# Two chunks of weights instead of one multiplied with the first half of the tokens as a stage opens

## The chip, the cores and the metric

The kernel runs on one core of one Trainium2 chip. The metric is the device time of one execution in microseconds; the median of three runs of the kernel before is 2975.34 us.

## What is computed

512 tokens of width 1024 go through four stages, each of which norms its input, multiplies it with wide weights and adds its result to the stream:

```python
h = rmsnorm(x, norm_mix_g)                      # stage 1, "mix"
proj = h @ w_in                                 # gated linear attention, sliding-window attention, gates
x = x + merged @ w_out
x = x + peer_layer(rmsnorm(x, norm_ffn_g), ...) # stage 2, "peer"
# peer: qp = xn @ w_pq ; top 16 of 128 keys per half and head ; 16384 experts, gelu, weighted sum
x = x + rms_norm(gated_deltanet(rms_norm(x, pre0)), post0)   # stage 3, "gdn"
x = x + rms_norm(short_conv(rms_norm(x, pre1)), post1)       # stage 4, "sconv"
# short_conv: u, b, c, z = split(h @ w_in, 4) ; (b * conv(c * u) * silu(z)) @ w_out
```

## The kernel before, in words

Matrix products are made nearly exact: a float32 operand is split into a high part (rounded for the matrix engine, PE) and a low part (what is left), and `mm3` (L210 to L212) issues three products, high x high, high x low, low x high.

Weights come in chunks of 1024 x 256, each in two parts that `wchunk` (L81) prepares: SP's queue loads a part into `wraw` (L91), the scalar engine (ACT) makes the high part `whi` (L92), and the vector engine (DVE) subtracts to get the low part `wlo` (L95). In some stretches every n-th part is subtracted by GpSimd (POOL); `share["every"]` is that n and 0 means never. In stage 1 it is 1 for the first chunk, in stage 3 it is 2 while the first products run, and in the openings of stages 2 and 4 it is 0. The pools hold three raw parts and three pairs of high and low parts, so a part's conversion waits until an earlier part has been used. These three instructions carry a priority of 4000 places ahead.

A slab is a buffer of 16 KB in each partition; there are seven, under one tag, and a slab goes to whichever tile is first written when one is free. A stage's stream holds four: `x`, the scaled tokens `x1s` to `x4s`, and the normed transposed tokens in high and low parts, `x1h`, `x1l` and so on.

As a stage opens, the 512 tokens come from the stage before in two halves of 256. `norm` (L171) takes a tile of 128 tokens: DVE scales it by its reciprocal root (L180; the root is made on POOL, L122 and L124), PE transposes it in blocks (L185), DVE multiplies by the gains (L188), ACT makes the high part (L190) and DVE the low part (L191). `first_feat` (L193) multiplies chunk 0: the first half of the tokens with both its parts (2 x 24 products of 256 columns), then the second half is normed if it isn't yet, then its 2 x 24 products. The later chunks go through `proj_feat`, 2 x 24 products of 512 columns each.

The instruction order on each engine is planned ahead of the run: a planner with a model of costs takes, on each engine, the earliest instruction in the program (with its priority) that is ready by that model. In stage 3 (and in parts of stage 1) PE's order is the program's own (`manual_schedule`). PSUM has five banks under the tag `ps` and three under `pp`; the products of a chunk go to `pp`.

What is made of the first results differs: stage 1 copies them (L314 to L316), stage 2 copies them (L855), multiplies with keys (L860) and selects the top 16 of each on DVE (L865 to L869), stage 3 convolves (L1070, L1072), stage 4 multiplies and convolves (L1697 on).

## Time and profile before

| | us |
|---|---|
| median of three runs | 2975.34 (2971.92 to 2978.11) |
| profiled execution | 2977.74 |
| its span on the core | 2976.0 |
| PE busy in the span | 2859.2 |
| DVE, ACT, POOL busy | 1978.8, 1213.2, 683.0 |
| mean granted clock of PE | 0.987 |

The span runs from the first to the last instruction. Busy times of different engines overlap. A wait of PE is time in which PE had an instruction in line whose data or buffer was not there; the row names the engine and line that released it last.

### The profile page before, as it was taken

Reading aid. Unit: us, or ns where it says so; the run is one execution under the profiler, and the core shown is the slowest. Engines: PE = TensorE matmul, PEld = TensorE weight load, DVE = VectorE, ACT = ScalarE, POOL = GpSimd, SP = SyncE. Lnnn points to the kernel's source line nnn. Section 1 sums busy time; section 2 is a strip of 40 time slices with the busy share of each in tenths; the row PEclk is TensorE's granted clock in tenths of the full one; section 3 lists DMA queues with packets and bytes.
Section 4 is the critical chain, followed back from the end, with each engine's and each line's share of the span. In section 5 each row is a group of like instructions: output and inputs, shape, how many; then the busy total and the mean of one; then the engine's idle time right before and its main releaser. Section 6 shows DMA issues by size and latency. Waiting matters only on the chain.

```text
span 2976.0 us, 43447 instructions
## 1 busy us (share of the span) xinstructions
PE 2859.2 (96%) x16530; PEld 2516.2 (85%) x16530; DVE 1978.8 (66%) x3806; ACT 1213.2 (41%) x2089; POOL 683.0 (23%) x592
## 2 busy tenths in 40 slices
PE   8999999999889998999999999999999998999998
PEld 6989778888789998888889898787878898888888
DVE  3357765499998875777788887757856665444432
ACT  3534573322355554333333333466344453323222
POOL 1000110001342311333545544125621212000000
PEclk9999999999999999999999999999999999999999
DMA  3214224322366777999999999535522423223222
GB/s 134 79 33 143 97 96 159 116 88 89 135 222 230 262 250 268 321 340 359 311 347 339 347 330 338 178 87 133 162 104 96 128 96 108 92 99 121 99 94 78
DMA packets 208076, 528.67 MB, mean 178 GB/s; under 512 B 39929, under 2 KB 85593, under 8 KB 203514
## 3 DMA queue, kind: packets, MB, share of 16 engines
q1 hardware_dynamic: 145170, 326.17, 33.1%
q0 software_dynamic: 43168, 155.27, 14.6%
q10 hardware_dynamic: 19528, 44.44, 4.1%
q8 instruction: 130, 2.13, 0.3%
q14 instruction: 80, 0.66, 0.1%
HBM read 464.49 MB, written 61.33 MB: 177 GB/s over the span
## 4 chain that ended last, share of the span: by engine, by line
PE 61%; DVE 5%; ACT 2%; DMA 1%; issue 1%; POOL 0%; ACTq 0%; DVEq 0%; POOLq 0%
PE pp L210 13%; PE pp L211 13%; PE pp L212 13%; PE ps L212 5%; PE ps L211 5%; PE ps L210 5%; PE ps L1517 2%; PE ps L968 1%; PE ps L969 1%; DVE wlo L95 1%; PE ps L1547 1%; DMA gath<-in_peer_u_rows_dram,ge 1%; PE ps L1566 1%; DVE AB L963 0%; ACT whi L92 0%
## 5 line engine op out<-in xcount | busy, mean ns | idle before, releaser
L92 ACT ACTIVATE whi<-wraw 128x1024 fp32r<-128x1024 f32 x492 | 519.1, 1056 | 847.0 <-PE pp L211 583.1
L95 DVE TENSOR_TENSOR wlo<-wraw,whi 128x1024 fp32r<-128x1024 f32 x466 | 583.0, 1251 | 349.1 <-ACT whi L92 338.7
L212 PE MATMUL pp<-x2h,wlo 128*128 128x384 f32 (+2 forms) x1168 | 402.7, 345 | 21.0 <-DVE wlo L95 19.4
L210 PE MATMUL pp<-x2h,whi 128*128 128x384 f32 (+2 forms) x1168 | 405.9, 348 | 15.1 <-ACT whi L92 8.7
L211 PE MATMUL pp<-x2l,whi 128*128 128x384 f32 (+2 forms) x1168 | 402.4, 345 | 0.8 <-DVE x2l L191 0.8
L212 PE MATMUL ps<-whi,wtl 128*128 128x512 f32 x640 | 252.7, 395 | 0.0
L211 PE MATMUL ps<-wlo,wth 128*128 128x512 f32 x640 | 252.6, 395 | 0.0
L210 PE MATMUL ps<-whi,wth 128*128 128x512 f32 x640 | 252.4, 394 | 0.0
L762 POOL DMA_INDIRECT gath<-in_peer_v_rows_dram,ge x128 | 181.7, 1420 | 306.4 <-DVE gath L765 153.8
L762 POOL DMA_INDIRECT gath<-in_peer_u_rows_dram,ge x128 | 182.2, 1424 | 296.5 <-DVE acc L770 144.5
L212 PEld LDWEIGHTS pp<-x2h,wlo 128*128 128x128 f32 x1168 | 223.4, 191 | 29.5 <-DVE wlo L95 22.9
L210 PEld LDWEIGHTS pp<-x2h,whi 128*128 128x128 f32 x1168 | 224.1, 192 | 21.7 <-ACT whi L92 9.4
L211 PEld LDWEIGHTS pp<-x2l,whi 128*128 128x128 f32 x1168 | 223.7, 192 | 6.5 <-DVE x2l L191 1.4
L210 PE MATMUL pp<-x4h,whi 128*128 128x512 f32 (+1 forms) x528 | 202.9, 385 | 3.8 <-ACT x4h L190 3.8
L211 PE MATMUL pp<-x4l,whi 128*128 128x512 f32 (+1 forms) x528 | 203.0, 385 | 0.6 <-DVE x4l L191 0.6
L212 PE MATMUL pp<-x4h,wlo 128*128 128x512 f32 (+1 forms) x528 | 202.8, 384 | 0.0
L830 ACT ACTIVATE wth<-wt 128x384 fp32r<-128x384 f32 x128 | 67.2, 525 | 330.8 <-PE pp L211 187.1
L770 DVE SCALAR_TENSOR_TENSOR acc<-gath,w,acc 128x1024 f32<-128x1024 f32 x127 | 162.5, 1279 | 25.4 <-DMA gath<-in_peer_v_rows_dram,ge 25.1
L765 DVE SCALAR_TENSOR_TENSOR gath<-gath,grow 128x1024 f32<-128x1024 f32 x128 | 157.3, 1237 | 33.0 <-DMA gath<-in_peer_u_rows_dram,ge 32.4
L210 PE MATMUL pp<-x3h,whi 128*128 128x512 f32 (+1 forms) x400 | 165.1, 413 | 7.4 <-ACT x3h L190 5.7
L211 PE MATMUL pp<-x3l,whi 128*128 128x512 f32 (+1 forms) x400 | 154.8, 387 | 1.6 <-DVE x3l L191 1.6
L212 PE MATMUL pp<-x3h,wlo 128*128 128x512 f32 (+1 forms) x400 | 154.9, 387 | 0.0
(498 smaller groups left out, 6534.9 us busy)
## 6 DMA issues: line engine op xcount, KB each, us to landing
wraw<-in_peer_u_dram SPq DMA_DIRECT2D x128, 512.0 KB
wraw<-in_peer_v_dram SPq DMA_DIRECT2D x128, 512.0 KB
wraw<-in_sc_w_in_dram SPq DMA_DIRECT2D x64, 512.0 KB
wraw<-in_w_in_dram SPq DMA_DIRECT2D x52, 512.0 KB
Gd<-sgs ACTq DMA_DIRECT2D x24, 1024.0 KB
wraw<-in_gdn_w_in_dram SPq DMA_DIRECT2D x48, 512.0 KB
Gt<-Gd SPq DMA_DIRECT2D x48, 400.0 KB
Hd<-ht ACTq DMA_DIRECT2D x25, 384.0 KB
```

The lines of the kernel that those rows point to most:

```text
L92: S.activation(hi, raw, AF.Copy)
L95: (GP if pool_ else V).tensor_tensor(lo, raw, f32(hi), op=ALU.subtract)
L210: PE.matmul(p, lh, rh, start=first, stop=False, skip_group_check=skip)
L211: PE.matmul(p, lh, rl, start=False, stop=False, skip_group_check=skip)
L212: PE.matmul(p, ll, rh, start=False, stop=last, skip_group_check=skip)
L762: GP.indirect_dma_start(out=r, out_offset=None, in_=src, in_offset=bass.IndirectOffsetOnAxis(ap=idx3[:, k:k + 1], axis=0))
L765: V.scalar_tensor_tensor(r, r, 1.0, xn3, op0=ALU.mult, op1=ALU.mult, accum_out=h3[:, k:k + 1])
L770: V.scalar_tensor_tensor(acc3, r, w3[:, k:k + 1], acc3, op0=ALU.mult, op1=ALU.add)
L830: S.activation(wh, w, AF.Copy)
L968: PE.matmul(o, AB[:, 1, :, q], A2[:, 0, :, q], start=True, stop=False)
L969: PE.matmul(o, AB[:, 1, :, q], A2[:, 1, :, q], start=False, stop=True)
L1517: PE.matmul(out_, RQ[s_][:, c:c + P], rhs, start=True, stop=True)
```

## The change

`first_feat` takes two chunks. Chunk 0's four parts go into one slab `wx`, and their low parts are always made on POOL; chunk 1's go through the small pool as before. The first half of the tokens is multiplied with both chunks (4 x 24 products of 256 columns), then the second half is normed, then it is multiplied with both. It is a generator now and hands out each result as it is finished; the fourth result lies in a bank of the tag `ps`. All four stages take their first four results from it. In stage 1 the line that set `share["every"]` is gone.

```diff
--- before.py
+++ after.py
@@ -78,20 +78,24 @@
     raws = {"of": [wraw], "n": 0}
-    def wchunk(ap, name="w"):
+    def wchunk(ap, name="w", into=None):
         for i in range(NK // HK):
             raws["n"] += 1
             raw = raws["of"][raws["n"] % len(raws["of"])].tile([P, HK * 256], F32, name=name + "raw", tag="wraw")
-            hi = wsp.tile([P, HK * 256], F32R, name=name + "hi", tag="whi")
-            lo = wsp.tile([P, HK * 256], F32R, name=name + "lo", tag="wlo")
+            if into is None:
+                hi = wsp.tile([P, HK * 256], F32R, name=name + "hi", tag="whi")
+                lo = wsp.tile([P, HK * 256], F32R, name=name + "lo", tag="wlo")
+            else:
+                hi, lo = into[:, 2 * i], into[:, 2 * i + 1]
             with tc.high_priority(offset=WPRIO):
                 nc.sync.dma_start(raw, ap[:, i * HK * 256:(i + 1) * HK * 256])
                 S.activation(hi, raw, AF.Copy)
                 share["n"] += 1
-                pool_ = share["every"] and share["n"] % share["every"] == 0
+                pool_ = into is not None or share["every"] and share["n"] % share["every"] == 0
                 (GP if pool_ else V).tensor_tensor(lo, raw, f32(hi), op=ALU.subtract)
             yield i, hi, lo
@@ -190,21 +194,25 @@
                 S.activation(h, p, AF.Copy)
                 V.tensor_tensor(l, p, f32(h), op=ALU.subtract)
-        def first_feat(self, ap, order=(0, 1)):
-
-            w = [(m, *kview(x, NK)) for m, *x in wchunk(ap)]
-            pp = [pj() for m in range(2)]
+        def first_feat(self, aps, order=(0, 1)):
+            wx = s16([P, 4, HK * 256], F32R, name="x%dw" % self.n)
+            w = [kview(x, NK) for ap, o in ((aps[0], wx), (aps[1], None)) for m, *x in wchunk(ap, into=o)]
+            w = [tuple(x) for x in w]
+            pp = [pj(), pj(), pj(), ps()]
             for j in order:
                 s = slice(256 * j, 256 * j + 256)
                 if j == order[1] and 2 * j not in self.normed:
                     self.norm(2 * j)
                     self.norm(2 * j + 1)
-                for m, wh, wl in w:
+                for p, (wh, wl) in zip(pp, w):
                     for k in range(NK):
-                        mm3(pp[m][:, s], wh[:, k], wl[:, k], self.h[:, k, s], self.l[:, k, s],
+                        mm3(p[:, s], wh[:, k], wl[:, k], self.h[:, k, s], self.l[:, k, s],
                             j == order[0] and k == 0, k == NK - 1, True)
-            return pp
+                    if j == order[1]:
+                        yield p
     def mm3(p, lh, ll, rh, rl, first, last, skip=False):
         PE.matmul(p, lh, rh, start=first, stop=False, skip_group_check=skip)
@@ -310,9 +318,9 @@
             gng = cl("gla_norm_g", [P, 2])
             xh, xl = X.h, X.l
             gqk = s16([P, 8, 512], name="gqk")
+            first2 = X.first_feat([w1[0], w1[1]])
             for c in range(4):
-                share["every"] = c == 0
-                for m, p in enumerate(proj_feat(w1[c], xh, xl) if c else X.first_feat(w1[0])):
+                for m, p in enumerate(proj_feat(w1[c], xh, xl) if c > 1 else (next(first2) for _ in range(2))):
                     S.activation(gqk[:, 2 * c + m, :], p, AF.Copy)
             wgh = cp.tile([P, NK * 16], F32R, name="wgh")
@@ -846,9 +854,10 @@
             tk = s16([P, 4, 1024], name="tk")
             v5 = lambda x: x.rearrange("p (t h m k) -> p t h m k", t=NT, h=8, m=2)
             top, itop = v5(tk[:, 0]), v5(tk[:, 1].bitcast(U32))
+            first2 = X.first_feat([A["w_peer_q"][0], A["w_peer_q"][1]])
             for h in range(8):
-                for m, p in enumerate(proj_feat(A["w_peer_q"][h], xh, xl) if h else
-                                      X.first_feat(A["w_peer_q"][0])):
+                for m, p in enumerate(proj_feat(A["w_peer_q"][h], xh, xl) if h > 1 else
+                                      (next(first2) for _ in range(2))):
                     if h == 0 and m == 0:
                         V.scalar_tensor_tensor(xn3, X.x[:, 3, :], X.rs[:, 3:4], grow, op0=ALU.mult, op1=ALU.mult)
                     q = tq.tile([P, T], F32, name="pq", tag="pq", bufs=2)
@@ -1115,8 +1124,8 @@
                 nonlocal gk
                 if i == 0:
-                    gk = iter(X.first_feat(w1[0], (1, 0)))
-                elif i % 2 == 0:
+                    gk = X.first_feat([w1[0], w1[1]], (1, 0))
+                elif i % 2 == 0 and i > 2:
                     gk = proj_feat_steps(w1[i // 2], xh, xl, NK)
                 return next(gk)
@@ -1692,13 +1701,14 @@
             xh, xl = X.h, X.l
             parts = [(s16([P, NK, T], F32R, name="sh%d" % i), s16([P, NK, T], F32R, name="sl%d" % i))
                      for i in range(2)]
+            first2 = X.first_feat([w1[0], w1[1]])
             for m in range(16):
-                p, p2 = proj_feat(w1[2 * m], xh, xl) if m else X.first_feat(w1[0])
+                p, p2 = proj_feat(w1[2 * m], xh, xl) if m else [next(first2) for _ in range(2)]
                 u = t2("scu")
                 S.activation(u, p, AF.Copy)
                 V.tensor_tensor(u, u, p2, op=ALU.mult)
                 acc = conv_silu(u, cw[:, m, :], 3, t2)
-                p, p2 = proj_feat(w1[2 * m + 1], xh, xl)
+                p, p2 = proj_feat(w1[2 * m + 1], xh, xl) if m else [next(first2) for _ in range(2)]
                 V.tensor_tensor(acc, acc, p, op=ALU.mult)
                 z = t2("scz")
                 S.activation(z, p2, AF.Silu)
```

## Rows read from the trace of the kernel before

**Rows 1.** The page's busy times: engine, busy us, share of the span, instructions.

```profile
PE 2859.2 (96%) x16530; PEld 2516.2 (85%) x16530; DVE 1978.8 (66%) x3806; ACT 1213.2 (41%) x2089; POOL 683.0 (23%) x592
```

**Rows 2.** Waits of PE, whole span: waiter, releaser, total us, times, longest us.

```profile
PE ps L185 <- DVE x4s L180: 5.9, 1, 5.9
PE pp L210 <- ACT x2h L190: 5.8, 2, 3.4
PE pp L210 <- ACT x3h L190: 5.7, 2, 4.4
PE pp L210 <- ACT x4h L190: 3.8, 2, 2.5
```

**Rows 3.** Timeline, stage 2 opening, PE: start, us, instruction, idle before.

```profile
583.30 0.80 PE L210 MATMUL pp<-x2h,whi 128*128 128x256 f32 x2 [3.38 <-ACT x2h L190]
...
591.98 1.91 PE L185 MATMUL ps<-ident,x2s 128*128 128x128 f32 x16
...
596.26 0.74 PE L210 MATMUL pp<-x2h,whi 128*128 128x256 f32 x3 [2.37 <-ACT x2h L190]
```

**Rows 4.** Timeline, stage 2 opening, DVE and ACT.

```profile
579.60 1.22 DVE L95 TENSOR_TENSOR wlo<-wraw,whi 128x1024 fp32r<-128x1024 f32 x1
...
587.78 1.42 DVE L180 TENSOR_SCALAR x2s<-x,x2rs 128x1024 f32<-128x1024 f32 x2 [1.11 <-POOL x2rs L124]
...
601.56 1.06 ACT L92 ACTIVATE whi<-wraw 128x1024 fp32r<-128x1024 f32 x1 [2.96 <-PE pp L211]
...
602.52 0.58 ACT L855 ACTIVATE pq<-pp 128x512 f32<-128x512 f32 x1
...
604.35 0.30 DVE L865 MAX8 tk<-ps 128x8 f32<-128x128 f32 x1 [0.48 <-PE ps L860]
...
604.57 1.21 DVE L95 TENSOR_TENSOR wlo<-wraw,whi 128x1024 fp32r<-128x1024 f32 x1
```

**Rows 5.** Timeline, stage 3 opening.

```profile
1919.24 2.36 POOL L95 TENSOR_TENSOR wlo<-wraw,whi 128x1024 fp32r<-128x1024 f32 x1 [1.34 <-ACT whi L92]
...
1920.47 2.22 DVE L95 TENSOR_TENSOR wlo<-wraw,whi 128x1024 fp32r<-128x1024 f32 x1
...
1929.82 1.42 DVE L180 TENSOR_SCALAR x3s<-x,x3rs 128x1024 f32<-128x1024 f32 x2 [2.02 <-POOL x3rs L124]
...
1933.80 1.91 PE L185 MATMUL ps<-ident,x3s 128*128 128x128 f32 x16
```

**Rows 6.** Timeline, stage 4 opening.

```profile
2523.76 1.42 DVE L180 TENSOR_SCALAR x4s<-x,x4rs 128x1024 f32<-128x1024 f32 x2 [1.75 <-POOL x4rs L124]
...
2527.26 1.91 PE L185 MATMUL ps<-ident,x4s 128*128 128x128 f32 x16
```

**Rows 7.** Timeline, stage 1 opening.

```profile
25.61 1.27 DVE L191 TENSOR_TENSOR x1l<-ps,x1h 128x512 fp32r<-128x512 f32 x2
...
28.97 0.40 PE L210 MATMUL pp<-x1h,whi 128*128 128x256 f32 x2
...
34.73 0.40 PE L210 MATMUL pp<-x1h,whi 128*128 128x512 f32 x1
```

**Rows 8.** Timeline, stage 4, PE: products of 512 columns.

```profile
2863.67 0.39 PE L211 MATMUL pp<-x4l,whi 128*128 128x512 f32 x1
...
2872.05 0.39 PE L212 MATMUL pp<-x4h,wlo 128*128 128x512 f32 x1
```

**Rows 9.** Timeline of SP's queue: issues of weight parts, x of them merged.

```profile
556.08 25.10 SPq L91 DMA_DIRECT2D wraw<-in_w_peer_q_dram  x6
...
1901.46 0.36 SPq L91 DMA_DIRECT2D wraw<-in_gdn_w_in_dram  x1
...
2484.53 27.09 SPq L91 DMA_DIRECT2D wraw<-in_sc_w_in_dram  x6
```

**Rows 10.** Windows: length, PE, PEld, DVE, ACT, POOL busy, clock, DMA, GB/s.

```profile
600.00:720.00 120.00, 120.00 (x636) 105.07 (x635) 112.31 (x619) 33.59 (x44) 0.86 (x1) 1.00 0.29 96
720.00:1000.00 280.00, 247.07 (x1501) 233.26 (x1500) 254.87 (x505) 127.21 (x154) 107.65 (x60) 0.98 0.55 190
```

## The prediction

> **What bounds the kernel now.** The page's busy times come first: the matrix engine is busy 2859.2 of 2976.0 us, so 116.8 us are idle on it and nothing can be won elsewhere unless it first makes PE wait less [rows 1]. The second view is PE's own waits. The openings of the stages stand in it by name: PE waits for the first normed tokens of stage 2 and again for the second, 5.8 us in two waits of which the longest is 3.4, so 3.4 and 2.4; in stage 3 4.4 and 1.3; in stage 4 5.9 (for the scaled tokens), 2.5 and 1.3 [rows 2]. The question for this change is which of these waits a second chunk can cover. I therefore read the timelines of the openings, PE first and then the engines that feed it.
>
> Stage 2 (peer): the first-half products of chunk 0 start at 583.30, the transposes of the second half follow them at 591.98 without any idle, and only after the transposes does PE stand for 2.37 us until 596.26 [rows 3]. The scaled second half was there at 587.78 + 1.42 = 589.2, 2.8 us before PE asked for it [rows 4]. Stage 3 (gdn): ready at 1929.82 + 1.42 = 1931.2, asked for at 1933.80, 2.6 us to spare [rows 5]. Stage 4 (sconv): ready at 2525.2, asked for at 2527.26, 2.1 us to spare [rows 6]. Stage 1 (mix): the last part of the second half is done at 25.61 + 1.27 = 26.9 and its products begin at 28.97 [rows 7]. So in all four openings one chunk already covers the making of the second half. What is idle lies before the first product (more work behind it does not help) and between the transposes and the second-half products.
>
> **The change, part by part.**
>
> *The split.* Chunk 1 is now done as two halves of 256 tokens, 96 products where there were 48 of 512. In stage 1 the 48 half-width products from 28.97 to 34.73 take 5.76 us, 0.12 apiece [rows 7]; a full-width one takes (2872.05 - 2863.67) / 37 = 0.2265, 37 steps lying between these two rows [rows 8]. So 2 x 0.12 - 0.2265 = 0.0135 us more for each of 48, 0.65 us an opening. This is added PE work on an engine that is the bound, with nothing to hide it.
>
> *The order.* The norm of the second half stands in the program behind all first-half products, now 96 and no longer 48; the planner takes the earliest instruction that is ready, and in stage 3 PE follows the program outright. So the transposes come 48 x 0.12 = 5.76 us later, the second half lies ready that much longer, and the wait between transposes and second-half products stays where it is, since nothing is left on PE to put in it. Value: 0. Bounds: at best these waits go altogether, 2.4 + 1.3 + 1.3 = 5.0 us [rows 2]; at worst they are what they are. In stage 2 the wait is 1.1 us longer than in the other two because the vector engine was on other work; that work now falls under the 5.76 us, so I take 1.1 off there.
>
> *The large buffer.* One slab of seven takes chunk 0's four parts. Counting the slabs in use at each opening (stage 2: two of the merged input, four of the stream; stage 3: the stream's and the last H and Gt; stage 4: two parts, Y and the stream's x until its s, h and l are written) leaves one free when the parts arrive. Value 0; the other end is a rival below. The weight slots that chunk 0 no longer takes are refilled by chunk 1 and the first part of chunk 2 at the same releases, so the conversions that sit in the openings stay: the vector engine's subtraction at 579.60 is then that of a later part [rows 4], the one at 1920.47 likewise [rows 5]. Value 0; were they gone from the chain to the first product, at best 1.22 + 2.22 and, counting stage 4 as two like the first, 2.4, together 5.8 us; at worst one more falls into the chain, 1.2 an opening.
>
> *The engine of chunk 0's subtraction.* In stages 2 and 4 both parts, in stage 3 one of two, move from DVE to POOL: five instructions of about 2.36 us where DVE takes 1.22 [rows 4, 5]. POOL also makes the reciprocal roots of the norms, so a part that runs at the wrong time would hold these. But the parts are loaded early: the DMA queue issues stage 2's from 556.08, stage 3's second at 1901.46, stage 4's from 2484.53 [rows 9], some 20 us before the first products, and no slot of the small pool has to come free first any more. Value 0. The bound is a collision: beside POOL's 2.36 us DVE's subtraction took 2.22 instead of 1.22, 1.0 us more [rows 4, 5]. Five collisions would be 5.0 us by that row, and five whole POOL instructions 11.8.
>
> The Trainium skill (SBUF — State Buffer, section "SBUF: two separate sides") holds that the port pair that VectorE and GpSimd share is an exclusive lock, so that the second to come is blocked for the whole of the other's instruction. The trace nearly agrees: the DVE instruction began at 1920.47 and ended 1.09 us after POOL's end at 1921.60. By that rule each collision could cost up to what POOL had left to run, and it speaks against moving these subtractions.
>
> *The results come later in stage 2.* There DVE is nearly the bound: 112.31 of 120 us from 600 to 720 and 254.87 of 280 from 720 to 1000, where PE has 33 us idle [rows 10]. Its selection chain starts with the first result of chunk 0, which now has 5.76 us of chunk 1 in front of it. Against that: 1.1 of the wait above; ACT's copy of that result, which stood behind a weight conversion that waited for PE until 601.56 and so came at 602.52, while its 24 products, back to back, would be done at 596.26 + 24 x 0.12 = 599.1 (3.4 us, since the conversions in front of it no longer wait for chunk 0's slots); and the subtraction at 604.57, 1.21 us, that is then done before [rows 4]. 5.76 - 1.1 - 3.4 - 1.21 = 0.05; I take 1.0, as not all of the ACT wait need go. Bounds: -1 (the wait and the split alone) and +5.8 (nothing is paid back). In this stage DVE sets the end, so the split isn't added.
>
> *Sum.* Stages 1, 3, 4: 3 x 0.65 = 1.95; stage 2: 1.0. Together +3.0 us. The profiled execution took 2977.74 (2976.0 of span and 1.7 around it), so it would take 2980.7; it lies 2.4 above the median of the runs, 2975.34, and the forecast for the median is 2978.3. About 0.2% (6 us) is what a measurement of this kernel can tell from no change, so this is "no change".
>
> **The rivals.**
>
> A, fast: the weight work leaves the openings, and the planner finds the transposes ready and puts them in front of chunk 1's products. Then up to 5.8 + 5.0 us go and 3.0 come: 2975.3 - 7.8 = 2967.5; with the 5.8 alone, 2972.5. For it: the waits are there and chunk 1's halves would fit them exactly. Against it: the transposes stand later in the program, PE never lacks a ready product in front of them, and in stage 3 the order is fixed. The planner also sees other times throughout and may order stage 2's tightly shared DVE better.
>
> B, slow: POOL's subtractions fall into the chains of the openings and hold the norm's roots and DVE. It decides as soon as chunk 0's parts reach POOL after about 574, 1916 and 2502. Price 5.0 (the measured collision) to 11.8, with the sum above: 2983 to 2990. Against it: the early DMA issues [rows 9].
>
> C, slow: stage 2's chain is pushed by the whole 5.76 and pays nothing back, 5.76 + 1.95 = 7.7: 2983.0. For it: DVE's 94% there [rows 10]. Against it: the ACT wait that goes.
>
> D: the change doesn't do what it says, since a slab is not free in time. In stage 4 the parts would wait for the slab of the scaled tokens, free at 2527.26 + 1.91 = 2529.2 [rows 6], then take a POOL instruction: some 13 us against a first product at about 2518.7 (after the wait of 2.5). About 2991.
>
> **How the numbers follow.** The forecast's own case 0.45, A 0.25, B 0.13, C 0.12, D 0.05. A is faster by over 0.2% only in its full form, but I leave it its whole 0.25 for a planner that gains in stage 2; B, C and D are 0.30. Range: 2967 (all of A) to 2990 (B's upper end), which leaves D and what is beyond A outside.
>
> **What would show it.** After the change PE should begin the second-half transposes 14 to 15 us after the first product in stage 2 (8.7 now), without idle in front, and should still stand 1 to 2.5 us behind them in stages 2, 3 and 4. Chunk 1 should show as half-width products, 0.12 us each. POOL's subtractions should lie before 574, 1916 and 2502, and the first product of each opening should follow the end of the stage before as it does now, within 1 us. The first selection instruction of stage 2 should be about 2 us later. I am wrong if the first product of an opening moves by more than 2 us, if transposes stand between chunk 0's and chunk 1's first halves, or if stage 2 changes by more than 4 us from its first product to its end.

## The result

The changed kernel takes 2999.97 us (median of 4 runs, 2997.86 to 3003.56) where the kernel before, run beside it, takes 2975.78. The ratio is 1.0081, 95% interval 1.0069 to 1.0094: 24 us slower. The forecast was 2978.3 and its range ended at 2990. The profiled execution took 2999.29 us, span 2997.5.

The page's busy times, columns as in [rows 1]: PE has 10.7 us more to do and 10.8 us more in which it does nothing (2997.5 - 2869.9 = 127.6, against 116.8).

```profile
PE 2869.9 (96%) x16722; PEld 2531.9 (84%) x16722; DVE 1966.5 (66%) x3801; ACT 1209.4 (40%) x2086; POOL 700.0 (23%) x597
```

PE's waits over the whole span, to be held against [rows 2]. The wait of L1201 (g_sums, the column sums of the gates in stage 3) was not there before; stage 4's waits have grown, stage 2's have shrunk (from 5.8 for x2h to 2.9, but 2.7 for x2s is new).

```profile
PE ps L189 <- DVE x4s L184: 7.1, 1, 7.1
...
PE ps L1201 <- DVE sma L1197: 5.4, 1, 5.4
PE pp L218 <- ACT x4h L194: 4.9, 2, 3.6
PE ps L1149 <- ACT l2sq L1139: 3.4, 2, 2.2
PE pp L218 <- ACT x2h L194: 2.9, 2, 1.6
...
PE ps L189 <- DVE x2s L184: 2.7, 1, 2.7
```

The opening of stage 2 on PE, the answer to [rows 3] (start, us, instruction, idle before): the second transposes now stand 15.0 us behind the first product, with no idle in front, and the waits behind them are still there. That is what the prediction said. What it did not say is the rate. The last two rows, half-width products one behind the other, start 0.22 us apart, not 0.12.

```profile
583.52 0.80 PE L218 MATMUL pp<-x2h,x2w 128*128 128x256 f32 x2 [1.58 <-ACT x2h L194]
...
598.54 1.91 PE L189 MATMUL ps<-ident,x2s 128*128 128x128 f32 x16
601.75 0.50 PE L218 MATMUL pp<-x2h,x2w 128*128 128x256 f32 x2 [1.31 <-ACT x2h L194]
...
604.61 0.41 PE L218 MATMUL pp<-x2h,x2w 128*128 128x256 f32 x1
604.83 0.41 PE L219 MATMUL pp<-x2l,x2w 128*128 128x256 f32 x1
```

The first selection instruction, in [rows 4] at 604.35, is 5.6 us later, and DVE sat idle for 5.14 us in front of it. ACT's copy of the first result, from which the selection is made, had waited for PE (ACT, then DVE):

```profile
608.11 0.60 ACT L864 ACTIVATE pq<-pp 128x512 f32<-128x512 f32 x1 [4.01 <-PE pp L220]
```

```profile
609.96 0.30 DVE L874 MAX8 tk<-ps 128x8 f32<-128x128 f32 x1 [5.14 <-PE ps L869]
```

POOL's subtractions of chunk 0, which the prediction had put ahead of 574, 1916 and 2502, are here (POOL, the openings of stages 2, 3 and 4; in this run the first transposes of stage 3 come 3 us later than before, those of stage 4 16 us later):

```profile
580.88 5.66 POOL L99 TENSOR_TENSOR x2w<-wraw,x2w 128x1024 fp32r<-128x1024 f32 x2 [6.08 <-ACT x2w L96]
...
1927.18 4.69 POOL L99 TENSOR_TENSOR x3w<-wraw,x3w 128x1024 fp32r<-128x1024 f32 x2
...
2534.20 5.66 POOL L99 TENSOR_TENSOR x4w<-wraw,x4w 128x1024 fp32r<-128x1024 f32 x2 [4.60 <-ACT x4w L96]
```

On ACT the conversions that feed them stand between the second and the third write of x4h, in stage 4 as in the two others. The large buffer was made in the middle of the opening, from parts that had been loaded long before (SP issued the stage's first two parts at 2499.30 and 2500.77):

```profile
2532.11 1.06 ACT L194 ACTIVATE x4h<-ps 128x512 fp32r<-128x512 f32 x2
2533.07 2.00 ACT L96 ACTIVATE x4w<-wraw 128x1024 fp32r<-128x1024 f32 x2
2535.09 1.20 ACT L194 ACTIVATE x4h<-ps 128x512 fp32r<-128x512 f32 x2
```

DVE beside POOL in stage 4: the same operation of the output projection takes 1.28 us before POOL starts and 2.08 beside it, and the last x4l for which PE waits comes after it.

```profile
2529.63 1.28 DVE L1064 SCALAR_TENSOR_TENSOR x<-ygY,yr,x 128x1024 f32<-128x1024 f32 x1 [0.58 <-POOL yr L128]
...
2535.56 2.08 DVE L1064 SCALAR_TENSOR_TENSOR x<-ygY,yr,x 128x1024 f32<-128x1024 f32 x1
2537.55 1.28 DVE L195 TENSOR_TENSOR x4l<-ps,x4h 128x512 fp32r<-128x512 f32 x2
```

The Trainium skill (SBUF — State Buffer, section "SBUF: two separate sides") has a GpSimd instruction that reads SBUF and a DVE instruction with two SBUF inputs exclude each other: whichever starts first has the port pair for its whole length. The trace fits that nearly in size. POOL's 5.66 us are 2.35 and 3.35. The DVE operation, with its inputs in SBUF, began when the first of them had 1.0 us left, and grew by 0.8; the second was 1.0 longer than the first. x4l, with one input in PSUM, keeps its 0.64 us apiece.

**Stage 3 on PE.** Five rows of the changed kernel. The transposes and the first wait of 1.3 us are as before; ab_mm (at 1955.09) stands 33.1 us behind the first transposes instead of 25.5; and then PE has nothing left to put ahead of g_sums:

```profile
1943.38 1.91 PE L189 MATMUL ps<-ident,x3s 128*128 128x128 f32 x16
1946.60 0.38 PE L218 MATMUL pp<-x3h,x3w 128*128 128x256 f32 x1 [1.31 <-ACT x3h L194]
...
1974.02 0.95 PE L1149 MATMUL ps<-ones,l2sq 128*128 128x1 f32 x8
1980.33 0.69 PE L1201 MATMUL ps<-sma,c_tri 128*128 128x64 f32 x2 [5.36 <-DVE sma L1197]
1980.78 0.78 PE L218 MATMUL pp<-x3h,whi 128*128 128x512 f32 x1
```

In the kernel before, g_sums has no wait:

```profile
1969.37 0.41 PE L1192 MATMUL ps<-sma,c_tri 128*128 128x64 f32 x2
```

The window behind the wait, columns as in [rows 10]: the granted clock is 0.68, a mixture of the levels 1.2 and 2.4 GHz. The 24 full-width products from 1980.78 take 8.15 us; at 2.4 GHz 24 of them take 24 x 0.2265 = 5.4 [rows 8].

```profile
1980.00:1990.00 10.00, 9.67 (x37) 8.03 (x38) 1.19 (x8) 4.17 (x7) 0.00 (x0) 0.68 0.03 12
```

The wait is the sum of two changes. PE has less to put between ab_tok and g_sums, since result 3 is 24 half-width products now: from 1964.35 to 1974.97, 10.6 us, where the kernel before had 13.1 (1956.25 to 1969.37). And the chain between them on ACT and DVE takes longer, 15.7 us to the start of sma's last step where it took 12.1 (DVE, before and changed):

```profile
1968.36 0.21 DVE L1188 SCALAR_TENSOR_TENSOR sma<-sma,alog 128x64 f32<-128x64 f32 x1
```

```profile
1980.06 0.21 DVE L1197 SCALAR_TENSOR_TENSOR sma<-sma,alog 128x64 f32<-128x64 f32 x1
```

2.5 and 3.6 us, less the 0.8 us that the kernel before had to spare, give 5.3 of the 5.36. Why the chain takes longer stands on ACT. A function table is loaded whenever the chain's exponentials and the results' Silu alternate, three times (1.28 us each) up to the chain's last exponential in the kernel before and four times here, as result 2's Silu (L1137) is now planned between two of the exponentials. A weight conversion of 1.06 us and its wait of 0.94 stand there too, at 1967.80 (ACT, before and changed):

```profile
1956.99 1.28 ACT L1175 ACT_TABLE_LOAD   x1
...
1958.96 1.28 ACT L1128 ACT_TABLE_LOAD   x1
...
1963.80 1.28 ACT L1182 ACT_TABLE_LOAD   x1
```

```profile
1965.20 1.28 ACT L1184 ACT_TABLE_LOAD   x1
...
1966.62 0.25 ACT L1185 ACTIVATE sme<-sma 128x64 f32<-128x64 f32 x1
...
1968.88 1.28 ACT L1137 ACT_TABLE_LOAD   x1
1970.17 0.63 ACT L1137 ACTIVATE kq<-cva 128x512 f32<-128x512 f32 x1
1970.83 1.28 ACT L1186 ACT_TABLE_LOAD   x1
1972.12 0.26 ACT L1186 ACTIVATE sme<-sme 128x64 f32<-128x64 f32 x1
...
1975.06 1.28 ACT L1191 ACT_TABLE_LOAD   x1
```

The Trainium skill (ScalarE: Activation LUTs, section "What ACT_TABLE_LOAD costs") gives 1283 ns for the load, which the trace has, and 1380 ns more for draining, which it doesn't: the load at 1970.83 begins 0.03 us after the end of the instruction ahead of it, and the one behind it starts 0.01 us after its end.

One window from the first transposes of stage 3 to the first step of the triangular solve (W), which waits for everything the gates feed, in the kernel before and in the changed one:

```profile
1918.88:2111.90 193.02, 181.62 (x997) 150.39 (x997) 130.28 (x255) 112.47 (x173) 72.69 (x64) 0.97 0.52 130
```

```profile
1922.00:2125.20 203.20, 187.84 (x1040) 157.78 (x1041) 124.41 (x254) 109.10 (x170) 75.76 (x65) 0.94 0.49 125
```

10.2 us more: 4.0 of idle (15.4 against 11.4) and 6.2 of PE busy, of which the split is 0.65. The other 5.6 go with a lower granted clock, 0.94 instead of 0.97.

### The profile page after: what moved, and what is told of

Same layout as the page of the kernel before. It is cut to its first block, busy times and chain, and to the rows that moved or that the text cites. A ratio compares the mean times of both kernels' runs of the same rounds, so it can differ in the third digit from the quotient of the medians.

```text
span 2997.5 us, 43833 instructions
## 1 busy us (share of the span) xinstructions
PE 2869.9 (96%) x16722; PEld 2531.9 (84%) x16722; DVE 1966.5 (66%) x3801; ACT 1209.4 (40%) x2086; POOL 700.0 (23%) x597
## 4 chain that ended last, share of the span: by engine, by line
PE 61%; DVE 4%; ACT 2%; issue 2%; DMA 2%; POOL 1%; POOLq 0%; DVEq 0%; SPq 0%; ACTq 0%
PE pp L218 13%; PE pp L219 13%; PE pp L220 13%; PE ps L220 5%; PE ps L219 5%; PE ps L218 5%; PE ps L1526 2%; PE ps L977 1%; PE ps L978 1%; PE ps L1556 1%; PE ps L1575 1%; DVE wlo L99 1%; DMA gath<-in_peer_v_rows_dram,ge 0%; DMA gath<-in_peer_u_rows_dram,ge 0%; ACT whi L96 0%
## 5 line engine op out<-in xcount | busy, mean ns | idle before, releaser
L99 DVE TENSOR_TENSOR wlo<-wraw,whi 128x1024 fp32r<-128x1024 f32 x461 | 572.6, 1242 | 357.3 <-ACT whi L96 356.5
L220 PE MATMUL pp<-x2h,wlo 128*128 128x384 f32 (+2 forms) x1136 | 391.3, 344 | 19.5 <-DVE wlo L99 17.7
L218 PE MATMUL pp<-x2h,whi 128*128 128x384 f32 (+2 forms) x1136 | 394.0, 347 | 10.2 <-ACT whi L96 8.8
L219 PE MATMUL pp<-x2l,whi 128*128 128x384 f32 (+2 forms) x1136 | 390.7, 344 | 0.0
L220 PEld LDWEIGHTS pp<-x2h,wlo 128*128 128x128 f32 x1136 | 216.5, 191 | 27.5 <-DVE wlo L99 21.4
L218 PE MATMUL pp<-x4h,whi 128*128 128x512 f32 (+1 forms) x496 | 191.4, 386 | 0.0
L219 PE MATMUL pp<-x4l,whi 128*128 128x512 f32 (+1 forms) x496 | 191.3, 386 | 0.0
L220 PE MATMUL pp<-x4h,wlo 128*128 128x512 f32 (+1 forms) x496 | 191.2, 386 | 0.0
L778 DVE SCALAR_TENSOR_TENSOR acc<-gath,w,acc 128x1024 f32<-128x1024 f32 x127 | 163.8, 1290 | 22.2 <-DMA gath<-in_peer_v_rows_dram,ge 21.7
L218 PE MATMUL pp<-x3h,whi 128*128 128x512 f32 (+1 forms) x368 | 154.7, 420 | 0.0
L220 PEld LDWEIGHTS ps<-whi,wtl 128*128 128x128 f32 x640 | 120.5, 188 | 28.9 <-DVE wtl L839 1.0
L219 PE MATMUL pp<-x3l,whi 128*128 128x512 f32 (+1 forms) x368 | 144.6, 393 | 0.0
```

The costliest lines, as they stand in the source:

```text
L99: (GP if pool_ else V).tensor_tensor(lo, raw, f32(hi), op=ALU.subtract)
L218: PE.matmul(p, lh, rh, start=first, stop=False, skip_group_check=skip)
L219: PE.matmul(p, lh, rl, start=False, stop=False, skip_group_check=skip)
L220: PE.matmul(p, ll, rh, start=False, stop=last, skip_group_check=skip)
L778: V.scalar_tensor_tensor(acc3, r, w3[:, k:k + 1], acc3, op0=ALU.mult, op1=ALU.add)
```

## The experiments

"Over" is the ratio to the kernel before, less one, times 2975.8 us, with its interval. For three stretches the trace gives a length: stage 2 from the first transposes to the last sgs, stage 3 from the first transposes to W, stage 4 from the first transposes to the last sh (us). The kernel before ran beside each, with medians from 2973.37 to 2975.86, so the second column alone doesn't rank the kernels.

| kernel | us | over, us | stage 2 | stage 3 | stage 4 |
|---|---|---|---|---|---|
| before | 2975.8 | 0 | 564.5 | 193.0 | 364.8 |
| changed | 2999.97 | 24.1 (20.5 to 28.0) | 570.8 | 203.2 | 369.2 |
| s3_only | 2987.43 | 12.2 (8.0 to 16.7) | 564.1 | 203.7 | 364.7 |
| s3_one | 2988.37 | 12.8 (8.9 to 16.7) | 570.6 | 198.5 | 369.1 |
| s2_only | 2978.64 | 6.5 (3.6 to 9.8) | 571.3 | 191.0 | 365.1 |
| s4_only | 2978.46 | 7.7 (4.8 to 10.4) | 564.5 | 192.4 | 369.0 |
| s3_sums_late | 2999.01 | 23.2 (19.0 to 27.4) | 570.5 | 203.7 | 369.2 |
| ab_first | 2999.73 | 25.9 (22.0 to 29.8) | 571.2 | 205.9 | 368.9 |
| lo_dve | 3003.35 | 29.5 (25.3 to 33.9) | 570.3 | 206.5 | 368.6 |
| early | 2994.39 | 17.3 (13.4 to 21.4) | 567.9 | 205.0 | 366.9 |
| norm_mid | 2988.45 | 14.6 (10.7 to 18.2) | 567.2 | 198.7 | 365.7 |
| act_after | 2993.16 | 17.9 (14.0 to 21.7) | 570.3 | 197.9 | 369.3 |
| joint | 2984.71 | 8.6 (5.1 to 12.2) | 564.3 | 203.1 | 363.3 |
| mid_early | 2981.30 | 5.4 (2.7 to 8.0) | 563.6 | 198.8 | 363.2 |
| mid_early_act | 2975.11 | 1.2 (-1.5 to 3.9) | 563.9 | 196.5 | 363.1 |
| two14 | 2973.17 | -2.4 (-5.1 to 0.3) | 563.9 | 192.2 | 363.0 |
| two124 | 2976.04 | 2.4 (-0.6 to 5.1) | 562.8 | 195.8 | 363.1 |

Each length is that of one execution. The six kernels with one chunk in stage 3 (before, s3_one, s2_only, s4_only, two14, two124) have 191.0 to 198.5 us there, so a difference of a few microseconds between two lengths of stage 3 needs the medians beside it.

**Which stage: s3_only, s3_one, s2_only, s4_only.** In these one chunk is multiplied with the first half, as in the kernel before, in the stages left out.

```diff
-                    gk = X.first_feat([w1[0], w1[1]], (1, 0))
-                elif i % 2 == 0 and i > 2:
+                    gk = X.first_feat([w1[0]], (1, 0))
+                elif i % 2 == 0:
```

> Two chunks in the third stage alone, one in the others. Theory 1 (the loss of 24.2 us lies for more than half in the third stage, where the trace of the changed kernel grows by about 13 us between its first transposes and its last L2 sums): 12 to 14 us above the kernel before, so 2988 to 2990 us, and the 5.4 us wait of g_sums for sma stands in its trace. Rival (each of the four openings loses about the same, the third stage shows more only because what the others lose surfaces there): about 6 us, 2982 us. My prediction's split alone would give 0.65 us, 2976.4 us.

> One chunk in the third stage, two in the others. Theory 1: 10 to 12 us above the kernel before (stage 2 about 3.5 to 4.8, stage 4 opening about 7 with what lies behind it, stage 1 -1.7), so 2985 to 2988 us; together with the kernel that has two chunks in the third stage alone the two surpluses should add up to the whole 24 us within 2 us. Rival (equal shares): 18 us, 2994 us.

> Two chunks in the second stage alone, as the change has it there, one in the others. The rest of the changed kernel (two chunks in stages 1, 2 and 4) measured 12.9 us over the kernel before. Theory: stage 2 costs what its first selection comes later, 5.7 us by the trace of the changed kernel (610.0 instead of 604.35, of which my sum had 1.0), less what the clock and the long middle give back: 3 to 6 us, 2979 to 2982 us. Rival (the selection's delay is absorbed by the products with the gathered rows, which have a queue of their own): 0 to 2 us, 2975.9 to 2978 us, and stage 4 carries the rest.

> Two chunks in the fourth stage alone, as the change has it there. Theory: 7 to 9 us over the kernel before, 2983 to 2985 us (in the changed kernel the transposes wait 7.1 instead of 5.9 us, the first products 3.6 and 1.4 instead of 2.5, the granted clock is 0.66 to 0.73 in two stretches, and 364.8 us from transposes to the last sh become 369.2). With stage 2 alone and the 1 to 2 us that stage 1 gives back, the three stages should add up to 12.9 us. Rival (the stages do not add): a sum of the single surpluses under 9 or over 17 us.

Stage 3 alone costs 12.2 us, stages 1, 2 and 4 together 12.8, stage 2 alone 6.5, stage 4 alone 7.7. 12.2 + 6.5 + 7.7 = 26.4 against 24.1 for the whole: the terms add within their intervals, and the -2 us left for stage 1 are not shown to be a gain. The traces don't show one either: stage 2's first transposes come between 574.8 and 578.0 us in the four kernels with one chunk in stage 1, and between 575.4 and 578.0 in those with two. The rival of equal shares falls. s3_one's stage 3 of 198.5 us is not explained: it has one chunk there, and its profiled run was 6 us above the median of its runs.

**The wait at g_sums: s3_sums_late, ab_first, act_after.** Three ways to give the gates' chain its time back. First, ask for its result later:

```diff
-            todo = {1: [ab_mm], 2: [ab_tok], 4: [g_sums], 5: [g_rows], ...
+            todo = {1: [ab_mm], 2: [ab_tok], 5: [g_sums], 6: [g_rows], ...
```

> The changed kernel with g_sums behind result 5 instead of 4 and g_rows behind 6 instead of 5, nothing else. Theory 1a (the list of side work is counted in results, and results 1 to 3 now come 2.9 us apart instead of 5.5, so the chain from ab_tok to g_sums has lost its cover; the stall of 5.4 us then lowers the granted clock to 0.68 and costs 2.6 us more): the wait at g_sums goes and so does the low clock behind it, 8 us less, about 2992 us. Rival 1b (half-width products and the clock are the price, the wait is only where it shows; the chain's next consumer waits instead, the transpose of g_rows or the rows of chunk 0): within 2 us of the changed kernel, 2998 to 3002 us.

The rival was right. The wait at g_sums is gone, W comes at 203.7 as without the edit, and PE waits elsewhere (from the first transposes to W; the first of these was 3.4 in the changed kernel, the two others are new):

```profile
PE ps L1149 <- ACT l2sq L1139: 3.9, 2, 2.0
PE pp L218 <- DVE cva L1081: 3.1, 2, 1.9
PE ps L1280 <- DVE rv L1270: 2.3, 1, 2.3
```

Second, start it earlier, ahead of the second halves:

```diff
-            todo = {1: [ab_mm], 2: [ab_tok], 4: [g_sums], ...
+            todo = {1: [ab_tok], 4: [g_sums], ...
-                    gk = X.first_feat([w1[0], w1[1]], (1, 0))
+                    gk = X.first_feat([w1[0], w1[1]], (1, 0), ab_mm)   # called as the second half opens
```

> The changed kernel with the products of the gate inputs (ab_mm) put ahead of the second halves of stage 3 instead of behind result 1, and ab_tok behind result 1 instead of 2; g_sums and g_rows stay behind results 4 and 5. Theory 3 (stage 3 is bound on two sides: TensorE, and the chain ab_mm, ab_tok, g_sums, g_rows, E, U, Cm, W, which in the kernel before starts 25.5 us after the first transposes and ends in W at 193.0, and in the changed kernel 33.1 and 203.2, because ab_mm stands behind 24 + 24 more half-width products; moving only g_sums later moved the wait to the next consumers): ab_mm starts at about 27 to 28 us, between ab_tok and g_sums lie 11 us of other products again, the wait at g_sums of 5.4 us is gone, W starts at 193 to 196; 7 to 10 us less than the changed kernel, 2990 to 2993 us. Rival (TensorE's own time: the products at half width and the clock windows behind each stall are the price, whichever stall it is): waits show up elsewhere in the stage, W stays at 201 to 204, within 2 us of the changed kernel, 2998 to 3002 us.

Right again for the rival, and my theory 3 falls: ab_mm starts at 24.4 us, but W comes at 205.9. PE now waits for the results' column sums, 10.7 us where it was 3.4. Four results at half width arrive within 12 us, and ACT has seven table loads, 9 us, between 1961 and 1986; the changed kernel has as many between 1956 and 1983, so the loads alone don't tell why.

```profile
PE ps L1151 <- ACT l2sq L1141: 10.7, 5, 4.0
```

Third, leave PE's order alone and let the chain go first on ACT and DVE:

```diff
+                    if i == 2:
+                        run(i)
                     sq[i] = kq_act(i, p)
                     run(i)
```

> The changed kernel with ab_tok's small operations recorded ahead of result 2's convolution and activation (the transposes of ab_tok stay at the same place on TensorE), nothing else. Theory 6 (the 5.4 us wait of g_sums is the chain on ACT and DVE between ab_tok and sma, 15.7 us instead of 11.7 in the kernel before, as result 2's Silu now falls between its exponentials and each change of function loads a table of 1.28 us; the products of results 3 and 4 cover only 10.7 us of it): with the chain ahead of result 2 on both engines the wait at g_sums falls from 5.4 to 0 to 2 us and W starts 4 to 7 us earlier; 2993 to 2996 us. Rival (ACT and DVE have as much work either way between 1955 and 1985, so the wait moves to the column sums on l2sq, as it did where ab_mm was put first): PE waits of the stage stay at 14 to 17 us, 2998 to 3002 us.

This one works: 6.2 us less than the changed kernel (17.9 against 24.1; the intervals just overlap, and the same edit on top of `mid_early` gives 4.2), W 5.3 us earlier, the wait at g_sums gone. The chain from ab_tok to sma's last step is down from 15.7 to 13.8 us. 3.0 us of the wait reappear one row ahead, so PE's idle time in the stretch falls by only 1.7 us (13.6 against 15.4); 3.6 us are PE's busy time, at a clock of 0.97 again.

```profile
1979.53 1.05 PE L1149 MATMUL ps<-ones,l2sq 128*128 128x1 f32 x8 [3.01 <-ACT l2sq L1139]
1980.73 0.43 PE L1201 MATMUL ps<-sma,c_tri 128*128 128x64 f32 x2
```

```profile
1924.80:2122.70 197.90, 184.26 (x1042) 154.45 (x1043) 129.15 (x254) 112.89 (x173) 75.09 (x65) 0.97 0.50 128
```

So theory 6 has the place and the time, and the rival has a point: more than half of the wait moved. Most of the gain in the stretch is PE's busy time, which goes with the clock.

**The late buffer: early, lo_dve.** In `early` chunk 0's slab, loads, conversions and subtractions are recorded ahead of the stage's first norm (stages 2, 3 and 4; in stage 3 the raw parts also go back to their first pool a little sooner):

```diff
                     if c == 3 and t:
+                        o.early()      # wx = s16(...); self.w0 = list(wchunk(ap, into=wx))
                         o.norm(0)
```

> The changed kernel with chunk 0's large buffer asked for, loaded, converted and subtracted ahead of the stage's first transposes in stages 2, 3 and 4 (in program order, ahead of the first norm), so that its two conversions on ACT and its two subtractions on POOL no longer stand between the first and the second pair of x_h writes. Theory 2a (slots of a tag are given out in program order of first writes, so that the early load of the changed kernel brought nothing, and the parts are made in the middle of the opening): stage 2 and stage 4 give back some 2 to 4 us each and stage 3 some 1 us, 2990 to 2995 us; DVE's subtraction in stage 4 falls from 2.08 back to about 1.28 us. Rival 2b (the parts were never what ended last, the openings wait for xs and x_l): within 2 us of the changed kernel. Rival 2c (the early parts hold up ACT and POOL in the evacuation of the output projection): 2 to 4 us slower, 3002 to 3004 us.

6.8 us less (17.3 against 24.1; the intervals overlap, but on top of `norm_mid` the same edit in stages 2 and 4 gives 9.2, clear of both), as theory 2a had it, though not by its parts: stage 2 gives 2.9, stage 4's stretch 2.3, and its wait ahead of the first transposes goes back from 7.1 to the 5.9 of [rows 2]; stage 3 gives nothing. The execution read here is the slowest of five, 8 us above their median. In stage 4 POOL starts 23 us ahead of the first transposes instead of 5.7 us behind them, and DVE's operation takes its 1.28 us again; PE, POOL and DVE in one fence each:

```profile
2534.72 3.65 PE L189 MATMUL ps<-ident,x4s 128*128 128x128 f32 x16 [5.92 <-DVE x4s L184]
```

```profile
2511.29 4.76 POOL L99 TENSOR_TENSOR x4w<-wraw,x4w 128x1024 fp32r<-128x1024 f32 x2 [1.31 <-ACT x4w L96]
```

```profile
2542.31 1.27 DVE L1077 SCALAR_TENSOR_TENSOR x<-ygY,yr,x 128x1024 f32<-128x1024 f32 x1
```

That the buffer's place in the program decides is shown by this. Whether the planner gives out the slots of a tag in the order of the program, as I argued, or whether its priorities work otherwise, the runs don't tell.

In `lo_dve` the late buffer stays late, and DVE subtracts (in stage 3 one of the two parts stays on POOL):

```diff
-                pool_ = into is not None or share["every"] and ...
+                pool_ = share["every"] and ...
```

> The changed kernel with the subtractions of chunk 0's large buffer on DVE instead of POOL (2 in each of 4 stages; in the first three stages' POOL share they follow the rule for other parts). Theory 5 (POOL's subtraction, 2.36 to 3.35 us, stands in the opening as the last thing before chunk 0's first products, and slows DVE beside it, 2.08 instead of 1.28 us in stage 4): DVE takes about 1.25 us each and the openings of stages 2 and 4 gain 1 to 2 us each, 2996 to 2998 us. Rival (DVE is the engine that ends the openings, with xs, the gains and x_l in its queue): 2.5 us more in the chain of each of the stages 2 to 4, 3003 to 3007 us.

5.4 us slower than the changed kernel (29.5 against 24.1), where the rival put it, but the intervals overlap, and stages 2 and 4 are no longer than the changed kernel's (570.3 and 368.6), which the rival doesn't have. Theory 5 falls; which engine is the better one in that place is not shown. Taking the subtraction off POOL gives nothing back there, making it early does.

**The waits behind the second transposes: norm_mid.**

```diff
-                if j == order[1] and 2 * j not in self.normed:
-                    self.norm(2 * j)
-                    self.norm(2 * j + 1)
-                for p, (wh, wl) in zip(pp, w):
+                for i, (p, (wh, wl)) in enumerate(zip(pp, w)):
+                    n = 2 * order[1]
+                    if j == order[0] and i == 2 and n not in self.normed:
+                        self.norm(n)
+                        self.norm(n + 1)
```

> The changed kernel with the transposes of the second half of the tokens put between the first halves of chunk 0 and of chunk 1 (stages 2, 3 and 4), so that chunk 1's first halves run while x_h and x_l are written. Theory 4 (in the changed kernel the second chunk's first halves stand ahead of the transposes, where nothing has to be covered: the waits of 1.3 and 0.4 to 0.8 us behind the second transposes stayed): those two waits go in three stages, and the first results, ab_mm among them, come as much earlier, 1.7 to 2.1 us in each stage, 5 to 6 us in all, 2994 to 2995 us. Rival (the second half's x_s is not ready at that place, as its norm waits for POOL's rs; the wait moves ahead of the transposes): within 2 us, 2998 to 3002 us.

9.5 us less (14.6 against 24.1, clear of both intervals), more than the 5 to 6 expected. In stage 3 the transposes are followed by a product at once; the two waits are gone:

```profile
1936.65 1.91 PE L189 MATMUL ps<-ident,x3s 128*128 128x128 f32 x16
1938.32 0.36 PE L218 MATMUL pp<-x3h,whi 128*128 128x256 f32 x1
```

The waits are 2.1 us of the 4.5 that stage 3 gives; in the stretch PE's idle time falls by 2.1 us (13.2 against 15.4) and its busy time by 2.4. g_sums still waits its 5.36 us, so this gain and act_after's are separate.

**Together: joint, mid_early, mid_early_act.**

> The changed kernel with three edits together: chunk 0's buffer early in stages 2 and 4, ab_mm ahead of the second halves in stage 3, the second transposes between the two chunks' first halves. If the three costs are separate they add: 5 + 7 to 10 + 5 us less than the changed kernel, 2980 to 2983 us. What is then left over the kernel before (5 to 8 us) would be the results of chunk 0 that come later in stages 2 and 4 (first selection and first scu wait for 48 more half-width products, 5.6 us). Rival (the costs share one cause, the low clock behind any stall, and do not add): 2988 to 2992 us.

> The changed kernel with the second transposes between the two chunks' first halves and chunk 0's buffer early in stages 2 and 4, without the move of ab_mm. If the two gains measured alone are separate (11.5 and 5.6 us), they add: 2981 to 2984 us. If the early buffer only shortened waits which the other order covers anyway: 2986 to 2989 us. Against the kernel with ab_mm moved as well (2984.7) this one shows what that move does in this order: by its trace (W at 203.1 us behind the first transposes with the move, at 198.7 without) it should be 3 to 4 us faster without it, 2981 us.

> All three edits that may help with two chunks in every stage: second transposes between the two chunks' first halves, buffer early in stages 2 and 4, ab_tok's small operations ahead of result 2's. If theory 6 holds: 2975 to 2979 us, level with the kernel before; if the wait only moves to the column sums: 2981 to 2984 us.

In these the buffer is early in stages 2 and 4 only. Adding the single gains, 9.5 + 6.8 + 6.2 = 22.5, and the three edits together give 24.1 - 1.2 = 22.9. `mid_early` alone: 18.7 for 16.3. They add, as far as intervals of some 4 us to either side can tell. `joint`, with the move of ab_mm that had failed by itself, stays 3 us above `mid_early`, in stage 3, as expected (the intervals overlap). With all three edits two chunks are level with the kernel before; stage 3 is still 3.5 us longer, which is no more than the lengths with one chunk differ, and stages 2 and 4 are 0.6 and 1.7 us shorter.

**A version to beat both: two14, two124.** Two chunks in stages 1 and 4 alone, in stage 4 with the buffer early and the transposes between the chunks; `two124` has stage 2 as well, made like stage 4.

> Two chunks in stages 1 and 4 alone (stage 4 with the early buffer and the second transposes between the two chunks), one chunk in stages 2 and 3 as in the kernel before. Theory: the stages whose results feed a chain on the other engines (stage 2's selection, stage 3's gates) lose by later results, the two others do not: stage 1 keeps its 1 to 2 us, stage 4 its 1 to 2 us (2523.2 to 2888.9, 365.7 us from transposes to the last sh in the one kernel, 363.3 in the other, 364.8 before): 2971 to 2974 us, 0.05 to 0.15% faster than the kernel before. Rival (any stage with two chunks loses): 2978 to 2982 us.

> Two chunks in stages 1, 2 and 4, with the buffer early in 2 and 4 and the second transposes between the chunks; one chunk in stage 3. If, with its buffer early and the waits covered, the second chunk costs stage 2 nothing (its first top-8 came at 603.7 in the kernel with both edits, 604.35 before): 2970 to 2973 us, level with or 1 to 3 us under the kernel with two chunks in stages 1 and 4 alone (2973.2). If the later results of stage 2 still count: 2975 to 2979 us.

two14 is faster than the changed kernel by 0.9%. Against the kernel before it is 0.9992 (0.9983 to 1.0001): 2.4 us, within what was expected, but no more than may be chance. two124 is not better: 1.0008 (0.9998 to 1.0017), though its stages 2 and 4 are as short; its stage 3, where both have one chunk, was longer by 3.6 us in the profiled run. Whether stage 2 gains or loses a microsecond or two by a second chunk stays open.

## Why the prediction was wrong

**The signs.** Of the signs of being wrong two came: from its first product to its last sgs stage 2 takes 563.6 us where it took 559.2, 4.4 more, and the waits ahead of stage 4's first product are 7.1 + 3.6 us where they were 5.9 + 2.5, 2.3 more.

**The split** (0.65 us a stage): the products are half-width, as said. 0.12 us each holds at 2.4 GHz only. Stage 2's 96 first halves took 15.0 us, 0.156 each, and those behind the second transposes partly 0.21. [rows 3] had shown it: there 48 first halves take 8.7 us, 0.18 each.

**The order** ("Value: 0 ... at worst they are what they are") is the step that failed most. Its picture was right in every row: transposes behind 96 products, 15.0 us after the first, no idle in front, the waits of 1.3 and 0.4 to 0.8 us still there, 1.1 us less of them in stage 2. Rival A's transposes between the chunks did not happen, for the reason given; norm_mid shows they would have been worth 9.5 us of the 24. But "at worst what they are" looked only at that wait. In stage 3 the list of side work counts results; all of them now come behind 48 more half-width products, and results 2 and 3 come 2.9 us apart instead of 5.5. I had read that PE follows the program outright there, and did not walk through the list that it follows. Stage 3 has 0.65 in my sum and measured 12.2: about 6 are the wait at g_sums and the clock behind it (act_after), some 4.5, by the lengths of one execution each, go with the transposes in the place that norm_mid corrects. What is left is within the noise. That the later start of the gates' chain costs anything by itself is not shown; starting it earlier (ab_first) gained nothing.

**The engine of chunk 0's subtraction** ("the parts are loaded early ... no slot has to come free first any more. Value 0") failed in the same way in stages 2 and 4. The raw parts were there; the buffer's conversions were planned behind the second x_h write all the same. Rival B named the right place, and its point of decision (POOL reached only after 574, 1916, 2502) is what the trace shows: 580.88, 1927.18, 2534.20. Its price, 5.0 to 11.8 us, holds `early`'s 6.8, but by luck: it was worked out from DVE slowed beside POOL, of which the openings of stages 2 to 4 show one case of 0.8 us, while ACT's conversions between the writes of x_h and the longer waits for x_s are in no rival. It had a chance of 0.13 because I took an early DMA for an early buffer.

**The results come later in stage 2** (1.0): measured 6.5 for the whole stage, near rival C's 5.8 of pushed chain. The 3.4 us to be paid back by ACT had been misread in [rows 4]. The conversion that ends its wait at 601.56 was released, by the order of the slots, by PE's last product with the first part, so the first result was not done at 599.1 but only about then. Its 24 products were not back to back: from 596.26 to 601.56 PE ran 37 (kernel before, columns as in [rows 10]), working at both results by turns.

```profile
596.26:601.56 5.30, 4.88 (x37) 4.56 (x38) 3.49 (x5) 0.60 (x2) 0.00 (x0) 1.00 0.00 0
```

Only the conversion itself, 0.96 us, stood between the result and its copy. In the changed kernel the copy waits for PE itself, whose products run partly at 0.21 us there. With the buffer early and the waits covered (mid_early) the first selection comes at 603.75, as early as before, in spite of 48 more products ahead of it, and the stretch is 563.6 against 564.5. So the second chunk need not delay the selection; what a delay alone costs, no run shows.

**The slab** was free: rival D did not happen, and `early` writes the slab 24.6 us ahead of stage 4's first transposes. B's place and C's size came together, with a stage 3 that no rival had; the range ended at B alone.

## What to carry over

Where an order written by hand counts in results, a change that alters how far apart results come changes every distance in it: walk through each entry, with the time from the operation that feeds it to the one that asks. Loading early is not having early: look for the instruction that turns the load into an operand, and for where it stands in its engine's queue. When a cover is added, put it behind the thing that makes one wait, not ahead of it. Before taking n products times the time of one for the time of a result, see whether PE works on that result alone.

## What was not expected of the hardware

What a wait of PE brings with it differs. In stage 3 5.36 us of waiting were followed by products that took 8.15 instead of 5.4 us; over the stretch 4.0 us of idle came with 5.6 us of lower clock (0.94 against 0.97). But behind the second transposes the kernel before and the changed one have the same waits of 1.3 and 0.8 us, and 24 + 24 half-width products behind them, once at a granted clock of 1.00 and once at 0.80; in `norm_mid`, without the waits, it is 1.00 (before, changed, `norm_mid`; columns as in [rows 10]):

```profile
1937.00:1944.42 7.42, 6.37 (x49) 5.96 (x49) 3.50 (x6) 2.23 (x3) 1.66 (x1) 1.00 0.00 0
```

```profile
1946.60:1955.10 8.50, 7.73 (x49) 7.36 (x50) 4.28 (x7) 1.29 (x2) 0.00 (x0) 0.80 0.01 2
```

```profile
1938.30:1951.00 12.70, 12.70 (x104) 12.14 (x103) 6.39 (x11) 3.68 (x7) 0.00 (x0) 1.00 0.05 17
```

Behind the same waits the clock was low in one kernel and not in the other; why is not shown. So there is no fixed price of a wait here, and norm_mid's 4.5 us for 2.1 us of waits in stage 3 is no such price: over the whole stretch its clock is 0.94, as in the changed kernel.

POOL's two subtractions take 5.66 us (2.35 and 3.35) in the openings of stages 2 and 4, where DVE runs an instruction with two SBUF inputs beside them, 4.69 in that of stage 3 and 4.76 outside the opening (`early`, stage 4), where it runs none.
